# A decoder layer in split fp32: query tiles one by one with one step of Strassen's products behind each, in place of pairs of tiles with up to three steps

## The chip, the cores and the metric

One NeuronCore of a Trainium2 chip. The metric is the device time of one execution in microseconds, the median of three runs: 1028.97 (1028.85 to 1028.97). One more execution was profiled; its trace is what the views below show. TensorE is called PE, its weight loads PEld, VectorE DVE, ScalarE ACT, GpSimd POOL, SyncE (which issues most of the loads) SP.

## What is computed

One decoder layer on x (256 tokens by 2048), fp32. Cut to what matters here:

```python
proj = jnp.einsum('btd,dc->btc', x, w_in[l])
(q_lat, c_kv, attn_gate, q_idx, k_idx, w_idx,
 x_rnn, rnn_gate, g_a, g_b) = jnp.split(proj, SPLIT_POINTS, axis=-1)
...
attn = _sparse_attention(q_lat, c_kv, q_idx, k_idx, w_idx, rel_bias, w_uv[l])
branch_a = jnp.einsum('btc,cd->btd', attn * jax.nn.silu(attn_gate), w_branch_a[l])
h = _rglru(x_rnn, conv_w[l], conv_b[l], w_gate_a[l], b_gate_a[l],
           w_gate_x[l], b_gate_x[l], lru_lambda[l])
branch_b = jnp.einsum('btc,cd->btd', h * jax.nn.silu(rnn_gate), w_branch_b[l])
merged = jax.nn.sigmoid(g_a) * branch_a + jax.nn.sigmoid(g_b) * branch_b
sub = jnp.einsum('btd,de->bte', merged, w_out[l])
x = _layernorm(ALPHA * x + sub, ln_g[l], ln_b[l])
```

`q_lat` has 16 heads of 256 columns, 32 tiles of 128 columns. The merge gates `g_a` and `g_b` have 2048 columns each, four chunks of 512.

## The kernel before

**Split products.** Every fp32 factor is split into a high part (`hi_of`, a copy on ACT, line 116) and a low part (`lo_of`, a subtraction on DVE, line 120), and a product is hi·hi + hi·lo + lo·hi. A weight piece of 128 x 1024 is loaded by SP into one of four buffers "raw" (512 KB), split into one of five buffers "hi" and one of five "lo", and used by PE. `halves` (line 183) is the list of all pieces in the order of use. `load_to(n)` and `split_to(n)` (lines 204 and 254) issue loads and splits up to piece n; the callers keep splits five pieces and loads nine pieces ahead of PE, which is what the buffers allow. Each engine executes its own instructions in the order in which the program emits them.

**The order of work.** `col_jobs` lists the stages: indexer queries (qi), attention gate (ag), queries (q), two chunks of gate A (ga), branch A (ba), RG-LRU input (xr), two chunks of gate B (gb), RG-LRU gate (rg), branch B (bb), then the output projection. Small work (evictions, the heads' softmax, sums) is written as generators on an agenda: `spawn(t, gen)` puts one at a tick, `tick(t)` runs what is due and moves it on at each `yield`. A tick is a quarter of a tile (eight matmuls) in the tile stages and six matmuls in the chunks. D0 is the first tick of the query stage.

**The query stage.** `pair` (line 1145) does two tiles of 128 columns together: eight runs of eight matmuls, first the four with the high weights (512 columns moving: x high and x low), then the four with the low weights (256 columns moving). The high and low buffers of a pair's four pieces come free in the last four runs. A tile's result is evicted by `post_q`, and `head(h)` (line 601) starts at D0 + 8h + 20: logits (`psl`, ten matmuls), softmax on DVE and ACT, transposes (`pspT`) nine ticks on, the product with the values (`pspv`) sixteen ticks on. `values(g)` (line 562) makes the values of four heads: twelve matmuls into two banks (`psv`), then a split on ACT (`vh`) and DVE (`vl`) in the next two ticks. It stands at the start of tile 8g + 6.

**Strassen's products in the query stage.** One chunk of gate A and one of gate B are computed not as chunks but by seven block products, four jobs of steps: j1 and j2 (eight steps of two products), j3 (four steps), j4 (eight). A step is six matmuls (`quarter_step`, line 943). `quarters(pair)` gives the steps behind each pair: 0, 0, 0, 2, 2, 2, 2, 0, 3, 3, 2, 2, 2, 3, 2, 3. The weight sums that they need are made by `sums` on DVE into eight tiles "form" or in the raw buffer; the sums of x by `early_sums`, and by `late_sum` (three operations on POOL with two scratch tiles, then a split) for j3. `quarter_sums` makes those for the next chunk, out of eight form tiles that `load_quarters` loads again over POOL's queue.

**Banks.** PSUM has eight banks: 0 to 3 for results of tiles and chunks (`accs`), 4 to 7 for the rest (`auxs`), each list used in rotation. While j1 to j4 run, bank 3 and bank 7 are taken out of the lists (at the first step) and hold the products; `after_j1` to `after_j4` (lines 968 to 1002) combine them, and after_j4 puts both banks back at the head of their lists.

Of the kernel before, what the change touches and what calls it, by code (L numbers as in the profile page):

```python
# [90 lines left out]
def layer(ctx, tc, ar, out):  # L93
# [90 lines left out]
    for job in jobs:  # L184
        if job[0] == "q" and job[1] % 8 == 6:
            where["uv", job[1] // 8] = len(halves)
            halves.append(("wuv", job[1] // 8, 0))
        for pc in range(8 if job[0] in CHUNKS else 2):
            step = seven(job) and (seven(job)[0], seven(job)[1][pc])
            if step and step[1] is not None:  # L190
                where[step] = len(halves)
                halves += [(step[0] + e, step[1], 0) for e in "ab"]
            where[job, pc] = len(halves)
            halves.append(("w" + job[0], job[1], pc) if job[0] in CHUNKS else ("wt", tiles.index(job), pc))
        if job[0] == "q" and job[1] % 2:
            for step in quarters(job[1] // 2):
                where[step] = len(halves)
                halves.append((*step, 0))
# [5 lines left out]
    def load_to(n):  # L204
        while st["load"] < min(n, len(halves)):
            i = st["load"]
            kind, a, s = halves[i]
            st["load"] += 1
            if kind in ("s1b", "s2b"):
                continue  # L210
            if kind == "s1a":
                nc.sync.dma_start(form[a], ar["wgb"][0, 4 + a // 2, :, a % 2, :])
            raw = wpool.tile([P, 1024], F32, name=f"raw{i}", tag="raw", bufs=4)
            raws[i] = raw
            if kind in ("j2", "j4"):
                src = ar["wgb"][3] if kind == "j2" else ar["wga"][2]
                nc.sync.dma_start(raw[:, :512], src[4 + a // 2, :, a % 2, :])
                continue
            if kind == "wt":
                src = ar["wt"][a, :, s * 8:(s + 1) * 8, :].rearrange("p k c -> p (k c)")  # L220
            elif kind == "j1":
                src = ar["wj"][a].rearrange("p k c -> p (k c)")
            elif kind == "j3":
                src = ar["wga"][2, a].rearrange("p k c -> p (k c)")
# [10 lines left out]
    def sums(i):  # L235


        kind, k, _ = halves[i]
        raw = raws[i]
        if kind == "j1":  # L240
            return nc.vector.tensor_sub(form[k], raw[:, 512:], raw[:, :512])
        if kind == "j2":
            return nc.vector.tensor_sub(form[k], raw[:, :512], form[k])
        if kind == "j3":
            for e in range(2):
                c = slice(e * 512, (e + 1) * 512)
                nc.vector.tensor_sub(raw[:, c], form[2 * k + e], raw[:, c])
            return
        if kind == "j4":
            return nc.vector.tensor_sub(raw[:, 512:], form[k], raw[:, :512])  # L250
        nc.vector.tensor_sub(raw[:, 512:], raw[:, 512:], raw[:, :512])
        nc.vector.tensor_sub(form[k], form[k], raw[:, 512:])

    def split_to(n):
        while st["split"] < min(n, len(halves)):
# [17 lines left out]
            else:  # L273
                if kind == "s1b":
                    raw = raws.pop(i - 1)
                    nc.vector.tensor_sub(raw[:, 512:], form[k], raw[:, :512])
                    src = [(slice(0, 512), form[k]), (slice(512, 1024), raw[:, 512:])]
                elif kind in ("j1", "j2"):
                    src = [(slice(0, 512), raws.pop(i)[:, :512]), (slice(512, 1024), form[k])]
                elif kind == "s2b":  # L280
# [568 lines left out]
    def load_quarters(n):  # L849

        x = []
        for j in range(8):
            x.append(gate_tile(f"form{n}_{j}", "form"))
            form[j] = x[j]
            nc.gpsimd.dma_start(x[j].rearrange("p (k t) -> p k t", k=2),
                                ar["xT"][2 * j:2 * j + 2].rearrange("k p t -> p k t"))
        return x
# [8 lines left out]
    def quarter_sums():  # L866

        x = load_quarters(1)
        yield 12

# [5 lines left out]
        for j in range(4):  # L876
            yield (1, 3, 4, 2)[j]
            dst = [p for tag in homes[j] for p in piece(tag, 2, 1 if tag in ("bias", "pa") else 2)]
# [19 lines left out]
    def early_sums():  # L898

        x = load_quarters(0)  # L900
        yield 16
        homes = {(s, j): slot(f"sj{s}_{j}").rearrange("p (k e t) -> p k e t", k=2, e=2)
                 for s, j in [(1, j) for j in range(4)] + [(s, j) for j in range(4) for s in (2, 4)]}
        for j in range(4):
            yield 3
            a11, a21, a12, a22 = four(x, j)
# [13 lines left out]
    def late_sum(j):  # L920

        d, e = (rows2(tmp_tile(f"s3{i}_{j}", "s")) for i in "de")
# [45 lines left out]
    def after_j1():  # L968
        for n, p in (("a", 1), ("c", 5)):
            cq[n] = gate_tile(f"cq_{n}")  # L970
            nc.scalar.activation(cq[n], psj[p], AF.Copy)
            yield 9

    def after_j2():

        cq["b"] = gate_tile("cq_b")
# [3 lines left out]
        yield 8  # L980
        cq["d"] = gate_tile("cq_d")
        nc.vector.tensor_add(cq["d"], psj[3], cq["c"])

    def after_j3():

        nc.vector.tensor_add(cq["b"], psj[7], cq["b"])
        yield
        nc.vector.tensor_add(cq["c"], psj[7], cq["c"])

    def after_j4():  # L990

        nc.vector.tensor_add(cq["a"], psj[2], cq["a"])
        yield
        nc.vector.tensor_sub(cq["b"], cq["b"], psj[4])
        accs.insert(0, 3)
        auxs.insert(0, 7)
        gates["gb", 3, 0], gates["gb", 3, 1] = cq["d"], cq["c"]
        yield 20
        for t, n in enumerate("ab"):
            gates["ga", 2, t] = cq[n]  # L1000
            nc.scalar.activation(cq[n], cq[n], AF.Sigmoid)
            yield
# [142 lines left out]
    def pair(kind, i):  # L1145

        t0 = at[kind, i]
        if kind == "q" and i % 8 == 6:
            spawn(t0, values(i // 8))
        pss = [acc_tile(f"ps_{kind}{i + e}") for e in range(2)]  # L1150
        for qt in range(8):
# [14 lines left out]
            if not high and half:  # L1166
                spawn(t + 1, posts[kind](i + e, pss[e]))
        if kind == "q":
            for job, k in quarters(i // 2):
                if (job, k) == ("j1", 0):  # L1170
                    accs.remove(3)
                    auxs.remove(7)
                quarter_step(job, k)
                if k == (3 if job == "j3" else 7):
                    spawn(t0 + 8, after[job]())

    for kind, i in jobs:
        if kind in CHUNKS:
            chunk(kind, i)
        elif i % 2 == 0:  # L1180
            pair(kind, i)
# [228 lines left out]
```

## Time and profile before

| | us |
|---|---|
| median of three runs | 1028.97 |
| profiled execution | 1027.56 |
| its span, first to last instruction | 1025.8 |
| PE busy | 1006.9 |
| DVE busy | 780.7 |
| ACT busy | 594.9 |
| POOL busy | 127.9 |
| mean granted clock of PE | 0.994 |

The query stage runs from 159.8 to 420.5 us of the span, gate A's two chunks follow. Rows of the view of waits read: who waited, `<-` for whom, us in total, times, longest. Rows of the timeline: start, duration, engine, line, operation, out<-in, and in brackets the idle time before it and what ended it. Rows of the windows: the stretch, its length, then busy us (and instructions) of PE, PEld, DVE, ACT and POOL, the granted clock, the busy share of the DMA engines and GB/s. Rows of groups: busy us, mean ns of one, and the idle time before. Rows of the chain: start, duration, what. Rows of loads: KB each and the median us from issue to landing.

### The profile page before, as it was taken

To read this page: it belongs to the slowest core of one execution; us is meant where nothing else is said; L and a number is where in the kernel's file an instruction comes from. 1 tells how busy PE (TensorE), PEld (TensorE's weight loads), DVE (VectorE), ACT (ScalarE), POOL (GpSimd) and SP (SyncE) were. 2 spreads that over 40 slices of the span, in tenths; PEclk is the share of its full clock that TensorE was granted. 3 is DMA by queue.
4 is the path that set the end of the run, shared out by engine and by line. 5 is a ranking of instruction groups with operands and counts; after the bars stand their busy time and mean duration, and the time that the engine had idled before them with its cause. 6 is when DMAs were issued, how large, how long until landed. Compare 5 with 4: busy or idle time off the path is not lost.

```text
span 1025.8 us, 14984 instructions
## 1 busy us (share of the span) xinstructions
PE 1006.9 (98%) x5320; PEld 867.4 (85%) x5320; DVE 780.7 (76%) x1306; ACT 594.9 (58%) x1014; POOL 127.9 (12%) x166
## 2 busy tenths in 40 slices
PE   9999999999999899799999999999999999999997
PEld 8898888888898788688888888888888888888885
DVE  5587887878778988658988868888678875655685
ACT  6566645666766566566555555555885554544452
POOL 0015341110102220300000000000252000000002
PEclk9999999999999999899999999999999999999999
DMA  9755886667556556745767676655555668766652
GB/s 307 252 165 177 307 309 204 191 186 241 166 177 195 185 166 203 266 144 191 220 217 217 204 230 188 191 191 192 179 182 166 202 211 327 224 185 184 195 175 82
DMA packets 65067, 210.08 MB, mean 205 GB/s; under 512 B 7120, under 2 KB 14160, under 8 KB 63968
## 3 DMA queue, kind: packets, MB, share of 16 engines
q1 hardware_dynamic: 61664, 195.32, 59.7%
q0 software_dynamic: 2608, 12.88, 3.4%
q8 instruction: 42, 0.69, 0.3%
q10 hardware_dynamic: 720, 0.92, 0.3%
q14 instruction: 33, 0.27, 0.1%
HBM read 206.96 MB, written 6.32 MB: 208 GB/s over the span
## 4 chain that ended last, share of the span: by engine, by line
PE 87%; DVE 5%; ACT 4%; issue 2%; DMA 1%; POOL 0%; DVEq 0%; ACTq 0%; POOLq 0%
PE ps_q L299 15%; PE ps_ag L299 9%; PE ps_xr L299 9%; PE ps_rg L299 5%; PE ps_ba L1096 3%; PE ps_bb L1096 3%; PE ps_bb L1095 3%; PE ps_ba L1097 3%; PE ps_ba L1095 3%; PE ps_bb L1097 3%; PE psq L299 2%; PE ps_qi L299 2%; PE pso L1095 2%; PE pso L1096 2%; PE pso L1097 2%; DVE lo L120 2%
## 5 line engine op out<-in xcount | busy, mean ns | idle before, releaser
L120 DVE TENSOR_TENSOR lo<-raw,hi 128x1024 fp32r<-128x1024 f32 x348 | 418.4, 1209 | 185.8 <-ACT hi L116 170.5
L116 ACT ACTIVATE hi<-raw 128x1024 fp32r<-128x1024 f32 x348 | 350.2, 1029 | 166.7 <-PE pso L1097 25.3
L299 PE MATMUL ps_q<-xs,hi 128*128 128x512 f32 x512 | 118.8, 389 | 0.0
L299 PEld LDWEIGHTS ps_q<-xs,hi 128*128 128x128 f32 x512 | 95.9, 188 | 19.8
L299 PE MATMUL ps_q<-xs,lo 128*128 128x256 f32 x512 | 69.2, 284 | 0.0
L299 PEld LDWEIGHTS ps_q<-xs,lo 128*128 128x128 f32 x512 | 65.2, 191 | 1.2
L299 PE MATMUL ps_rg<-xs,hi 128*128 128x512 f32 x256 | 60.2, 391 | 0.6 <-ACT hi L116 0.6
L299 PE MATMUL ps_ag<-xs,hi 128*128 128x512 f32 x256 | 60.0, 390 | 0.0
L299 PE MATMUL ps_xr<-xs,hi 128*128 128x512 f32 x256 | 59.6, 390 | 0.0
L299 PEld LDWEIGHTS ps_rg<-xs,hi 128*128 128x128 f32 x256 | 47.5, 188 | 11.0 <-ACT hi L116 1.5
L299 PEld LDWEIGHTS ps_xr<-xs,hi 128*128 128x128 f32 x256 | 47.6, 188 | 9.6
L299 PEld LDWEIGHTS ps_ag<-xs,hi 128*128 128x128 f32 x256 | 47.5, 188 | 9.5
L556 POOL TENSOR_TENSOR bias<-bias,mask 128x256 f32<-128x256 f32 (+1 forms) x32 | 27.0, 865 | 191.4 <-DMA bias<-dz 75.1
L1095 PE MATMUL ps_bb<-hi,ub 128*128 128x512 f32 x128 | 50.4, 393 | 0.0
L1097 PE MATMUL ps_ba<-hi,ua 128*128 128x512 f32 x128 | 49.9, 390 | 0.0
L1096 PE MATMUL ps_ba<-lo,ua 128*128 128x512 f32 x128 | 49.9, 390 | 0.0
L1097 PE MATMUL ps_bb<-hi,ub 128*128 128x512 f32 x128 | 49.9, 390 | 0.0
L1096 PE MATMUL ps_bb<-lo,ub 128*128 128x512 f32 x128 | 49.9, 389 | 0.0
L1095 PE MATMUL ps_ba<-hi,ua 128*128 128x512 f32 x128 | 49.8, 389 | 0.0
L1095 PE MATMUL pso<-hi,xs 128*128 128x512 f32 x96 | 37.5, 391 | 0.0
L1097 PE MATMUL pso<-hi,xs 128*128 128x512 f32 x96 | 37.4, 389 | 0.0
L1096 PE MATMUL pso<-lo,xs 128*128 128x512 f32 x96 | 37.4, 389 | 0.0
(424 smaller groups left out, 2062.9 us busy)
## 6 DMA issues: line engine op xcount, KB each, us to landing
raw<-in_wt SPq DMA_DIRECT2D x168, 512.0 KB, 4.8
raw<-in_wba SPq DMA_DIRECT2D x32, 512.0 KB, 3.8
raw<-in_wbb SPq DMA_DIRECT2D x32, 512.0 KB, 4.3
raw<-in_wo SPq DMA_DIRECT2D x32, 512.0 KB, 3.5
raw<-in_wga SPq DMA_DIRECT2D x20, 512.0 KB, 4.0
raw<-in_ws SPq DMA_DIRECT2D x16, 512.0 KB, 4.5
raw<-in_wgb SPq DMA_DIRECT2D x16, 512.0 KB, 4.0
wr<-in_wA SPq DMA_DIRECT2D x14, 424.0 KB, 4.9
```

The lines of the kernel that those rows point to most:

```text
L116: nc.scalar.activation(hi, src, AF.Copy)
L120: nc.vector.tensor_sub(lo, src, f(hi))
L299: nc.tensor.matmul(ps[:, :n], w, rhs[:, :n], start=start, stop=stop)
L556: nc.gpsimd.tensor_add(b[:, r, :W[r]], b[:, r, :W[r]], mask[:, r, :W[r]])
L1095: nc.tensor.matmul(o, mh, hi, start=first and d == 0, stop=False)
L1096: nc.tensor.matmul(o, mh, lo, start=False, stop=False)
L1097: nc.tensor.matmul(o, ml, hi, start=False, stop=d == KT - 1)
```

## The change

- Query tiles are done one by one by `single`: high, low, low, high runs of eight matmuls, so that each piece is done with before the next.
- One step of Strassen's products stands behind each tile from tile 5 on, and one behind tile 3.
- The steps of j2 and j4 share loads: the even step loads 512 KB for itself and the odd one (before: 256 KB each). j4 makes its difference in the form tile and splits two halves of 512 columns.
- The results of j1 are kept in two "slot" tiles, and the gates get tiles of their own when their values exist; after_j4 puts bank 7 at the end of the list, and banks 3 and 7 leave the lists at tile 0.
- `load_quarters` issues its eight loads two at a time, three ticks apart; early_sums starts at D0 - 30 in place of D0 - 16.
- `values` moves to the start of tile 8g + 4, `head` starts two ticks earlier, late_sum uses one scratch tile and other ticks, the constants of the RG-LRU come 30 ticks later, and the POOL multiplications in `roots` are spread.

The diff, cut to its core:

```diff
-def quarters(pair):
+def quarters(i):
-    n = (0, 0, 0, 2, 2, 2, 2, 0, 3, 3, 2, 2, 2, 3, 2, 3)
-    return steps[sum(n[:pair]):sum(n[:pair + 1])]
+    return steps[:1] if i == 3 else steps[i - 4:i - 3] if i > 4 else []
...
-        if job[0] == "q" and job[1] % 8 == 6:
+        if job[0] == "q" and job[1] % 8 == 4:
             where["uv", job[1] // 8] = len(halves)
...
-            if kind in ("s1b", "s2b"):
+            if kind in ("s1b", "s2b") or kind in ("j2", "j4") and a % 2:
                 continue
...
-                nc.sync.dma_start(raw[:, :512], src[4 + a // 2, :, a % 2, :])
+            elif kind in ("j2", "j3", "j4"):
+                src = {"j2": ar["wgb"][3, 4 + a // 2], "j3": ar["wga"][2, a], "j4": ar["wga"][2, 4 + a // 2]}[kind]
...
         if kind == "j4":
-            return nc.vector.tensor_sub(raw[:, 512:], form[k], raw[:, :512])
+            return nc.vector.tensor_sub(form[k], form[k], half)
...
         nc.vector.memset(w[:, :, 0:1], 1.0)
+        yield 6 * q
         for n in range(4 * q, 4 * q + 4):
-            yield
+            yield 2 if q else 1
             nc.gpsimd.tensor_mul(v[:, n, :], v[:, n, :], ri[n][:, T:])
...
+        for m in range(4):
+            for j in (m, m + 4):
+                nc.gpsimd.dma_start(rows2(x[j]), ar["xT"][2 * j:2 * j + 2].rearrange("k p t -> p k t"))
+            yield 3
...
-        nc.gpsimd.tensor_sub(e, x[2], x[3])
-        nc.gpsimd.tensor_add(d, d, e)
+        nc.gpsimd.tensor_add(d, d, x[2])
+        nc.gpsimd.tensor_sub(d, d, x[3])
...
     def after_j1():
         for n, p in (("a", 1), ("c", 5)):
-            cq[n] = gate_tile(f"cq_{n}")
+            cq[n] = slot(f"cq_{n}", F32)
             nc.scalar.activation(cq[n], psj[p], AF.Copy)
-            yield 9
+            yield
...
     def after_j4():
-        nc.vector.tensor_add(cq["a"], psj[2], cq["a"])
-        yield
+        c11 = gates["ga", 2, 0] = gate_tile("ga2_0")
+        nc.vector.tensor_add(c11, psj[2], cq["a"])
         nc.vector.tensor_sub(cq["b"], cq["b"], psj[4])
         accs.insert(0, 3)
-        auxs.insert(0, 7)
+        auxs.append(7)
...
-    spawn(D0 - 16, early_sums())
-    for j, pair in enumerate((11, 11, 12, 12)):
-        spawn(D0 + 8 * pair - (4 if j < 2 else -1) + j % 2, late_sum(j))
-    spawn(at["ga", 0] + 3, quarter_sums())
+    spawn(D0 - 30, early_sums())
+    for j, t in enumerate((76, 79, 83, 87)):
+        spawn(D0 + t, late_sum(j))
+    spawn(at["ga", 0] + 2, quarter_sums())
...
-    spawn(D0 + 20, lru_consts())
+    spawn(D0 + 50, lru_consts())
...
-        spawn(D0 + 8 * h + 20, head(h))
+        spawn(D0 + 8 * h + 18, head(h))
...
+    def single(i):
+        t0 = at["q", i]
+        if i % 8 == 4:
+            spawn(t0, values(i // 8))
+        if i == 0:
+            accs.remove(3)
+            auxs.remove(7)
+        ps = acc_tile(f"ps_q{i}")
+        for qt, high in enumerate((True, False, False, True)):
+            t, half = t0 + qt, qt // 2
+            seams(t)
+            n = where[("q", i), half]
+            w = parts[n][0 if high else 1]
+            for kk in range(8):
+                mm(ps, w[:, kk * P:(kk + 1) * P], xs[:, half * 8 + kk, :], high, qt + kk == 0, qt == 3 and kk == 7)
+            if qt % 2:
+                parts.pop(n)
+            tick(t)
+            split_to(n + (6 if qt % 2 else 5))
+            load_to(n + (10 if qt % 2 else 9))
+        spawn(t0 + 4, post_q(i, ps))
+        for job, k in quarters(i):
+            quarter_step(job, k)
+            if k == (3 if job == "j3" else 7):
+                spawn(t0 + 4, after[job]())
```

More of the change, by code (lines that the diff above doesn't have):

```diff
@@ L194, in layer @@
             halves.append(("w" + job[0], job[1], pc) if job[0] in CHUNKS else ("wt", tiles.index(job), pc))
-        if job[0] == "q" and job[1] % 2:
-            for step in quarters(job[1] // 2):
+        if job[0] == "q":
+            for step in quarters(job[1]):
                 where[step] = len(halves)
@@ L214, in load_to @@
             raws[i] = raw
-            if kind in ("j2", "j4"):
-                src = ar["wgb"][3] if kind == "j2" else ar["wga"][2]
-                nc.sync.dma_start(raw[:, :512], src[4 + a // 2, :, a % 2, :])
-                continue
             if kind == "wt":
@@ L222, in load_to @@
                 src = ar["wj"][a].rearrange("p k c -> p (k c)")
-            elif kind == "j3":
-                src = ar["wga"][2, a].rearrange("p k c -> p (k c)")
+            elif kind in ("j2", "j3", "j4"):
+                src = {"j2": ar["wgb"][3, 4 + a // 2], "j3": ar["wga"][2, a], "j4": ar["wga"][2, 4 + a // 2]}[kind]
+                src = src.rearrange("p k c -> p (k c)")
             elif kind in ("s1a", "s2a"):
@@ L238, in sums @@
         kind, k, _ = halves[i]
+        if kind in ("j2", "j4") and k % 2:
+            i = next(n for n in reversed(range(i)) if halves[n][:2] == (kind, k - 1))
         raw = raws[i]
+        half = raw[:, k % 2 * 512:(k % 2 + 1) * 512]
         if kind == "j1":
@@ L242, in sums @@
         if kind == "j2":
-            return nc.vector.tensor_sub(form[k], raw[:, :512], form[k])
+            return nc.vector.tensor_sub(form[k], half, form[k])
         if kind == "j3":
@@ L277, in split_to @@
                     src = [(slice(0, 512), form[k]), (slice(512, 1024), raw[:, 512:])]
-                elif kind in ("j1", "j2"):
+                elif kind == "j1":
                     src = [(slice(0, 512), raws.pop(i)[:, :512]), (slice(512, 1024), form[k])]
+                elif kind in ("j2", "j4"):
+                    n = i if k % 2 == 0 else next(n for n in reversed(range(i)) if halves[n][:2] == (kind, k - 1))
+                    raw = raws.pop(n) if k % 2 else raws[n]
+                    src = [(slice(0, 512), raw[:, k % 2 * 512:(k % 2 + 1) * 512]), (slice(512, 1024), form[k])]
                 elif kind == "s2b":
@@ L849, in load_quarters @@
     def load_quarters(n):
[L851 to L856, printed above, removed]
+        x = [gate_tile(f"form{n}_{j}", "form") for j in range(8)]
+        form.update(enumerate(x))
+        for m in range(4):
+            for j in (m, m + 4):
+                nc.gpsimd.dma_start(rows2(x[j]), ar["xT"][2 * j:2 * j + 2].rearrange("k p t -> p k t"))
+            yield 3
         return x
@@ L866, in quarter_sums @@
     def quarter_sums():
-        x = load_quarters(1)
-        yield 12
+        x = yield from load_quarters(1)
         def piece(tag, bufs, n=1):
@@ L876, in quarter_sums @@
         for j in range(4):
-            yield (1, 3, 4, 2)[j]
+            yield (2, 3, 4, 2)[j]
             dst = [p for tag in homes[j] for p in piece(tag, 2, 1 if tag in ("bias", "pa") else 2)]
@@ L898, in early_sums @@
     def early_sums():
-        x = load_quarters(0)
-        yield 16
+        x = yield from load_quarters(0)
+        yield 8
         homes = {(s, j): slot(f"sj{s}_{j}").rearrange("p (k e t) -> p k e t", k=2, e=2)
@@ L904, in early_sums @@
         for j in range(4):
-            yield 3
+            yield 2
             a11, a21, a12, a22 = four(x, j)
@@ L920, in late_sum @@
     def late_sum(j):
-        d, e = (rows2(tmp_tile(f"s3{i}_{j}", "s")) for i in "de")
+        d = rows2(tmp_tile(f"s3d_{j}", "s"))
         x = [f(xs[:, 2 * j:2 * j + 2, c:c + P]) for c in (0, P, T, T + P)]
         nc.gpsimd.tensor_sub(d, x[0], x[1])
-        nc.gpsimd.tensor_sub(e, x[2], x[3])
-        nc.gpsimd.tensor_add(d, d, e)
+        nc.gpsimd.tensor_add(d, d, x[2])
+        nc.gpsimd.tensor_sub(d, d, x[3])
         yield 2
@@ L969, in after_j1 @@
         for n, p in (("a", 1), ("c", 5)):
-            cq[n] = gate_tile(f"cq_{n}")
+            cq[n] = slot(f"cq_{n}", F32)
             nc.scalar.activation(cq[n], psj[p], AF.Copy)
-            yield 9
+            yield
     def after_j2():
-        cq["b"] = gate_tile("cq_b")
+        cq["b"] = gates["ga", 2, 1] = gate_tile("ga2_1")
         nc.vector.tensor_add(cq["b"], psj[6], cq["a"])
@@ L979, in after_j2 @@
         nc.gpsimd.tensor_add(cq["c"], cq["c"], cq["b"])
-        yield 8
-        cq["d"] = gate_tile("cq_d")
-        nc.vector.tensor_add(cq["d"], psj[3], cq["c"])
+        yield 2
+        gates["gb", 3, 0] = gate_tile("gb3_0")
+        nc.vector.tensor_add(gates["gb", 3, 0], psj[3], cq["c"])
     def after_j3():
@@ L987, in after_j3 @@
         yield
-        nc.vector.tensor_add(cq["c"], psj[7], cq["c"])
+        gates["gb", 3, 1] = gate_tile("gb3_1")
+        nc.vector.tensor_add(gates["gb", 3, 1], psj[7], cq["c"])
     def after_j4():
-        nc.vector.tensor_add(cq["a"], psj[2], cq["a"])
-        yield
+        c11 = gates["ga", 2, 0] = gate_tile("ga2_0")
+        nc.vector.tensor_add(c11, psj[2], cq["a"])
         nc.vector.tensor_sub(cq["b"], cq["b"], psj[4])
         accs.insert(0, 3)
-        auxs.insert(0, 7)
-        gates["gb", 3, 0], gates["gb", 3, 1] = cq["d"], cq["c"]
+        auxs.append(7)
         yield 20
-        for t, n in enumerate("ab"):
-            gates["ga", 2, t] = cq[n]
-            nc.scalar.activation(cq[n], cq[n], AF.Sigmoid)
+        for g in (c11, cq["b"]):
+            nc.scalar.activation(g, g, AF.Sigmoid)
             yield
@@ L1147, in pair @@
         t0 = at[kind, i]
-        if kind == "q" and i % 8 == 6:
-            spawn(t0, values(i // 8))
         pss = [acc_tile(f"ps_{kind}{i + e}") for e in range(2)]
@@ L1167, in pair @@
                 spawn(t + 1, posts[kind](i + e, pss[e]))
[L1168 to L1175, printed above, removed]
+    def single(i):
[23 more added lines that the diff above has]
+                spawn(t0 + 4, after[job]())
     for kind, i in jobs:
@@ L1179, in layer @@
             chunk(kind, i)
+        elif kind == "q":
+            single(i)
         elif i % 2 == 0:
```

## The prediction

> **What bounds the kernel now.** I read the engine table of the page first:
>
> ```profile
> PE 1006.9 (98%) x5320; PEld 867.4 (85%) x5320; DVE 780.7 (76%) x1306; ACT 594.9 (58%) x1014; POOL 127.9 (12%) x166
> ```
>
> TensorE (PE) is busy 1006.9 of 1025.8 us. The change adds and removes no matmul, so it can only move the 18.9 us in which PE stands, and the clock that PE is granted. The view of waits, for PE alone, says where PE stands:
>
> ```profile
> PE psl L305 <- DVE cq_b L994: 5.2, 1, 5.2
> PE pspv L650 <- DVE vl L120: 2.8, 1, 2.8
> PE psj L961 <- DVE pb L120: 1.3, 1, 1.3
> PE psj L962 <- DVE lo L120: 1.1, 1, 1.1
> ...
> PE ps_rg L299 <- ACT hi L116: 0.6, 1, 0.6
> ```
>
> The first four lie in the query stage or at its end and make 10.4 us. Next the windows, for the load of the query stage and the granted clock (the column behind POOL) around the longest wait:
>
> ```profile
> 140.00:159.80 19.80, 19.80 (x121) 17.68 (x120) 13.31 (x28) 9.79 (x16) 3.62 (x4) 1.00 0.89 314
> 213.90:420.50 206.60, 202.49 (x1165) 178.41 (x1164) 168.68 (x343) 132.88 (x281) 36.20 (x43) 1.00 0.60 189
> 428.00:432.00 4.00, 0.11 (x1) 0.00 (x0) 2.21 (x5) 3.09 (x9) 0.00 (x0) 0.79 0.96 373
> 432.00:434.00 2.00, 0.67 (x3) 0.67 (x4) 1.27 (x4) 1.81 (x5) 0.00 (x0) 0.50 0.91 306
> 434.00:436.00 2.00, 2.00 (x10) 1.96 (x10) 1.89 (x3) 1.16 (x3) 0.26 (x1) 0.50 0.44 116
> 436.00:438.00 2.00, 2.00 (x9) 1.71 (x8) 2.00 (x5) 0.53 (x2) 1.87 (x2) 0.71 0.84 213
> ```
>
> The means of 0.79, 0.50, 0.50 and 0.71 are a half clock for 1.7 + 2 + 2 + 1.2 = 6.8 us, from about 430.3 to 437.2. In the 206.6 us before it, with a wait of 2.8 us in them, the clock stays at 1.00. So the half clock belongs to the 5.2 us wait, and costs on top of it half of the time that PE works at it. These rows of the timeline give that time, and the cause:
>
> ```profile
> 427.72 0.39 PE L1097 MATMUL ps_ga<-hi,xs 128*128 128x512 f32 x1
> 433.33 0.58 PE L305 MATMUL psl<-cT,qs 128*128 128x256 f32 x1 [5.22 <-DVE cq_b L994]
> ```
>
> ```profile
> 425.42 1.06 ACT L116 ACTIVATE hi<-raw 128x1024 fp32r<-128x1024 f32 x1 [4.20 <-DMA raw<-in_wga]
> 428.70 1.06 ACT L116 ACTIVATE hi<-raw 128x1024 fp32r<-128x1024 f32 x1 [2.22 <-DMA raw<-in_wga]
> ```
>
> ```profile
> 416.54 5.82 POOL L855 DMA_DIRECT2D form<-in_xT  x8
> ```
>
> PE works from 433.3 to 437.2 at half clock: 3.9 us, 1.9 us lost. The recoverable total is 10.4 + 1.9 = 12.3 us.
>
> **The change, part by part.** The pace of PE comes from the chain of waits between two waits, where each piece is PE itself:
>
> ```profile
> 229.86 8.21 PE ps_q L299 x40
> ...
> 238.77 0.47 PE psl L608 x4
> 239.25 0.23 PE pspv L650
> 239.47 0.12 PE pspv L651
> ...
> 239.82 0.96 PE ps_q L299 x8
> 240.78 0.11 PE pspT L633
> 240.89 0.22 PE pspT L635 x2
> ```
>
> Eight low matmuls are 0.96 us, so the 32 high ones in the first row are 8.21 - 0.96 = 7.25 us: 1.81 us a run of eight, 0.227 us each. A psl is ten matmuls of 0.12 (1.2 us), a pspv 0.23 + 3 x 0.12 = 0.6, a pspT 0.33.
>
> *Tiles one by one.* 32 high and 32 low matmuls become four runs of high, low, low, high. Low runs of eight already stand between psl and pspT in these rows and cost no more per matmul than 0.12, so I put the changes of width at zero. What changes is when the five hi/lo buffers come free: now four of them within the 3.84 us of low runs, then none for 7.25 us; after, one per 1.81 + 0.96 = 2.8 us. Splits and loads follow at the same even pace, and one step of Strassen's products (six matmuls, 1.4 us) stands behind each tile instead of none to three behind each pair.
>
> DVE has to keep up. In 213.9 to 420.5 it is busy 168.7 us for twelve pairs with 26 steps: 14.1 us a pair against 202.5 / 12 = 16.9 us of PE, 83%. With two steps a pair both fall a little, and the share stays. DVE pays a little more for the fourth job: one split of 1024 columns becomes two of 512 there.
>
> ```profile
> L120 DVE TENSOR_TENSOR lo<-raw,hi 128x1024 fp32r<-128x1024 f32 x348 | 418.4, 1209 | 185.8 <-ACT hi L116 170.5 <-PE ps_q L299 10.4 <-issue 3.3
> L116 ACT ACTIVATE hi<-raw 128x1024 fp32r<-128x1024 f32 x348 | 350.2, 1029 | 166.7 <-PE pso L1097 25.3 <-DMA raw<-in_wt 24.4 <-PE ps_bb L1097 24.3
> ...
> L120 DVE TENSOR_TENSOR lo<-form,hi 128x512 fp32r<-128x512 f32 x32 | 22.2, 693 | 0.1
> ...
> L120 DVE TENSOR_TENSOR vl<-psv,vh 128x512 fp32r<-128x512 f32 x8 | 5.1, 678 | 0.4 <-ACT vh L116 0.4
> ```
>
> That is 8 x (2 x 0.693 - 1.209) = 1.4 us over eight tiles, under DVE's 17% of slack; uncovered it would cost at most those 1.4 us.
>
> *The four waits.* (1) 5.2 + 1.9 us: after_j4 put bank 7 at the head of the auxiliary list, so the next psl took it although DVE's read of it (L994) was queued behind splits that waited for loads; those loads shared the DMA engines with eight form loads that POOL had issued in one go. After, bank 7 goes to the end of the list, and the form loads go two at a time, the later ones behind the last bias addition on POOL's queue. Two loads of 256 KB (128 x 512 x 4 bytes) in three quarters of six 0.227 us matmuls each (3 x 1.37 us) ask 128 GB/s; the gate's own 512 KB per 2.73 us ask 192; together 320, below the 373 GB/s that the window shows. I take all 7.1 us as gone. (2) 1.3 us: the first step took bank 7 from a pspT still being read. It now leaves the list at tile 0, sixteen quarters ahead: gone. (3) 1.1 us: late_sum's last hi/lo came late. Its split is now emitted five to six quarters ahead of its step, in place of three to four for the two late ones, with one scratch tile instead of two in tag "s"; its three POOL operations remain three: gone. (4) 2.8 us: with three auxiliary banks the pspv of head 4g-1 reuses the first psv bank of group g, and waited for vl:
>
> ```profile
> 337.98 0.58 ACT L116 ACTIVATE vh<-psv 128x512 fp32r<-128x512 f32 x1
> ```
>
> ```profile
> 342.13 0.67 DVE L120 TENSOR_TENSOR vl<-psv,vh 128x512 fp32r<-128x512 f32 x1
> ```
>
> ```profile
> 342.86 0.50 PE L650 MATMUL pspv<-pa,vh 128*128 128x512 f32 x1 [2.75 <-DVE vl L120]
> ```
>
> This one doesn't go; it moves. After, values() stands at tile 8g+4 and head starts two quarters earlier, so psv, psl, pspv follow in this order again and pspv of head 4g-2 reuses the bank. vl is emitted after the tile's first low run, and the bank is wanted one low run and one psl later: 0.96 + 1.2 = 2.1 us. Now it is two high runs, a low run and a psl: 5.8 us. What stands ahead of vl on DVE, counted from the last psv matmul: the next split, which needs ACT's 1.03 and then 1.21 us; one 256-column addition, half of the 0.69 row or a little more, 0.4; vl's first half, 0.68; in all 3.3 us. PE arrives after 1.81 + 0.96 + 0.96 + 1.2 = 4.9 us. So a DVE that is 1.6 us behind costs nothing, and each further microsecond costs one, three times (g = 1, 2, 3; at g = 0 there is no such head). At g = 1 two copies of after_j1 stand ahead of vh on ACT or right behind it, at g = 2 an addition of after_j2 stands ahead of vl; both cost about 0.7 of that margin. Bounds: 0, and the lag that the row shows now, below in the rivals. DVE at 83% in an even order is nearer to the first: 0.5 us each, 1.5 us.
>
> *The hand-over of banks 3 and 7 between jobs.* Each job now follows the one before it in the next tile. The last result of j1 or j3 is emitted after quarter 1 of the next tile and its bank is wanted after a low and a high run, psl, pspv, pspT and three matmuls: 0.96 + 1.81 + 1.2 + 0.6 + 0.33 + 0.7 = 5.6 us, 4.9 without the 0.68 of the reading itself; from j2 to j3 5.2. Bounds again zero and today's lag; I take 0.3 us in all.
>
> *Loads.* Eight of 256 KB fewer for each of two jobs, eight of 512 KB more, same bytes. The odd step issues no load, and its even neighbour's raw buffer is held over one tile more, so loads still run four pieces ahead. Cost zero, if the 2.8 us pace of splits covers a later landing (rivals).
>
> *The rest.* Half of early_sums, twelve operations of 256 columns on DVE at about 0.4 us (the estimate above), 5 us, moves into the end of the previous stage, where DVE is idle 19.8 - 13.3 = 6.5 us and PE never waits; without that cover it would cost those 5 us. cq in slots instead of gates: a place in memory. lru_consts later, quarter_sums' pauses: the same operations on the same engines. In roots POOL's multiplications spread out, and the first comes one quarter later, with the scan of DVE behind it; the nearest rows are PE's 0.6 us wait in that stage, which may go, and one low run, 0.96, which may be added. I take zero for all of these.
>
> Sum: 12.3 - 1.5 - 0.3 = 10.5 us. The profiled execution took 1027.56 us (span 1025.8 and 1.8 around it), which would become 1017.1; it stood 1.4 under the median, so the median goes from 1028.97 to **1018.5 us**.
>
> On the clock, the Trainium skill (TensorE: Matmul & The Clock Gate, Part 1) lets the half clock end one window of about 3.4 us after work resumes, which makes 1.7 us lost instead of the 1.9 that the rows give; by that the sum is 10.3.
>
> **The rivals.**
>
> *B, late loads.* The landing times are
>
> ```profile
> raw<-in_wj SPq DMA_DIRECT2D x8, 512.0 KB, 3.6
> raw<-in_wgb SPq DMA_DIRECT2D x8, 256.0 KB, 2.9
> ```
>
> so each of eight doubled loads lands 0.7 us later, and with one raw buffer held nothing may hide it: 5.6 us, 1024.1. For it speaks ACT's 4.20 us wait for a load above; against it the DMA share of 0.60 in the query stage.
>
> *C, the slower side: bank hand-over with DVE behind.* vl was due after the second high run of its pair, at 330.6 + 3.6 = 334.2 (the first starts as the last psv ends), and ran at 342.13: 7.9 us behind. If that lag stays, each of three values waits 7.9 + 0.7 - 2.1 = 6.5 us and, being longer than 5.2, also pays 1.9 us of half clock; the hand-overs add 3.0, 2.7 and 3.0. That is 34 us of new waits: 1028.97 - 12.3 + 34 = 1051 us. The point from which it decides is a lag of about 5.2 us, where 3 x 3.8 and 0.7 of hand-overs eat the 12.3. For it: that lag, and the 2.1 us in place of 5.8. Against: the lag arose where ACT and DVE stood for loads while four pieces came due at once.
>
> *D, the wait at the gates is only renamed.* If the gate's loads still land late, PE waits for its own pieces of the gate instead of bank 7, and 7.1 us come back: 1025.6; with another few of these it is no change.
>
> *E.* If more frequent changes of bank made PE idle in short gaps often enough to lose its clock, say once per pair, sixteen times 1.9 us would bring 1018.5 + 30 = 1049. Against it: in 213.9 to 420.5 PE changes its bank with every psl, pspv and step, at 1.00. The same page of the Trainium skill (A second HAM failure mode: psum-queue depth-cycling) describes such a loss in another kernel; no row here shows it.
>
> **How the numbers follow.** Forecast (1016.2 to 1021) 0.70; B 0.08; D 0.10; C 0.10; E 0.02. The low end is the whole 12.3 us and the 0.6 of ps_rg, 1016, less a little: 1015.5. The high end takes in B and D: 1026. C, E and the tail of D stay out. About 0.2%, 2.1 us, can be told from no change: below 1026.9 lie the forecast, B and 0.06 of D, 0.84; above 1031.0 most of C and E, 0.11; between them 0.05.
>
> **What would show it.** Right: PE's waits have no cq_b and no psj rows over 0.5 us, pspv <- vl is at most 1 us three times, the clock of every window between the start and the tail is 1.00, and PE's busy time is about 1005. Wrong: psl or pspv waiting for vl over 2 us (C), ACT waiting for in_wga or in_wgb loads with ps_q waiting for it (B), ps_ga waiting for lo at the start of the gates (D), a clock under 1.00 without a long wait (E).

## The result and the profile after

| us | before | after |
|---|---|---|
| median, with its range | 1028.91 (1027.25 to 1028.97, 4 runs) | 1020.39 (1017.44 to 1020.91, 4 runs) |
| profiled execution | 1027.56 | 1020.15 |
| its span | 1025.8 | 1018.4 |

The ratio is 0.9915, with a 95% interval of 0.9894 to 0.9937: 8.5 us less in the medians, 7.4 in the spans. The forecast was 10.5 us less. The engine table after:

```profile
PE 1006.4 (99%) x5320; PEld 867.4 (85%) x5320; DVE 785.1 (77%) x1314; ACT 597.6 (59%) x1022; POOL 131.9 (13%) x166
```

PE now stands for 1018.4 - 1006.4 = 12.0 us (before 18.9), and is busy 0.5 us less: together the 7.4. The view of waits of PE says which of the four long waits are gone:

```profile
PE pspv L653 <- DVE vl L119: 4.0, 1, 4.0
PE warm L315 <- DVE eps L166: 1.0, 1, 1.0
PE ps_rg L302 <- ACT hi L115: 0.6, 1, 0.6
```

No cq_b, no psj. (The second row is at the kernel's start, the third in the RG-LRU gate.) One wait is left in the query stage, and it has grown from 2.8 to 4.0 us. The windows: the query stage, the gates after it, then two windows of 3.41 us around that wait.

```profile
213.90:420.50 206.60, 202.62 (x1158) 177.77 (x1157) 173.33 (x359) 134.44 (x290) 36.48 (x39) 0.99 0.61 188
420.50:440.00 19.50, 19.50 (x100) 16.58 (x99) 13.78 (x27) 11.93 (x26) 6.34 (x8) 1.00 0.79 255
323.17:326.58 3.41, 0.41 (x2) 0.36 (x3) 3.41 (x6) 1.64 (x3) 1.25 (x2) 1.00 0.40 120
326.58:329.99 3.41, 3.41 (x11) 2.80 (x10) 3.41 (x5) 0.38 (x1) 3.25 (x5) 0.50 0.67 205
```

At the gates, where PE stood 5.2 us and had a half clock, it is busy 19.50 of 19.50 us at full clock. The new half clock follows the wait for vl and costs 3.41 / 2 = 1.7 us. So the wait costs 4.0 + 1.7 = 5.7 us: nearly half of the 12.3 us that the old waits and their half clock had cost.

Its cause stands in the timelines of DVE ahead of vl, of ACT (which makes vh, the half that vl needs), of SP and of PE:

```profile
313.57 2.23 DVE L246 TENSOR_TENSOR raw<-form,raw 128x512 f32<-128x512 f32 x2
315.73 1.21 DVE L119 TENSOR_TENSOR lo<-raw,hi 128x1024 fp32r<-128x1024 f32 x1
...
317.93 2.35 DVE L119 TENSOR_TENSOR lo<-raw,hi 128x1024 fp32r<-128x1024 f32 x2
322.15 1.29 DVE L246 TENSOR_TENSOR raw<-form,raw 128x512 f32<-128x512 f32 x2 [1.87 <-DMA raw<-in_wga]
323.36 1.22 DVE L119 TENSOR_TENSOR lo<-raw,hi 128x1024 fp32r<-128x1024 f32 x1
324.50 0.68 DVE L980 TENSOR_TENSOR ga<-psj,cq_a 128x512 f32<-128x512 f32 x1
325.10 0.41 DVE L389 TENSOR_TENSOR s_q<-ps_q,r_q 128x256 f32<-128x256 f32 x1
325.43 1.28 DVE L119 TENSOR_TENSOR vl<-psv,vh 128x512 fp32r<-128x512 f32 x2
```

```profile
319.80 1.07 ACT L115 ACTIVATE vh<-psv 128x512 fp32r<-128x512 f32 x2
```

```profile
316.97 0.33 SPq L225 DMA_DIRECT2D raw<-in_wga  x1
```

```profile
317.12 1.98 PE L302 MATMUL ps_q<-xs,hi 128*128 128x512 f32 x8
318.94 2.07 PE L302 MATMUL ps_q<-xs,lo 128*128 128x256 f32 x16
...
326.17 0.50 PE L653 MATMUL pspv<-pa,vh 128*128 128x512 f32 x1 [3.98 <-DVE vl L119]
```

The row of 322.15 is `sums` for j3's second step, in the order well ahead of vl. Its load left SP at 316.97, when a raw buffer came free (the split of 315.73 ends at 316.94), and DVE stood for it 1.87 us; the two sums, a split and two more operations came between its landing and vl. vh was ready at 320.9, so it was DVE that held vl. The last psv matmul ends at 317.12, where the ps_q run starts. By the prediction's count vl was due 3.3 - 0.68 = 2.6 us later, at 319.7; it ran at 325.43, 5.7 us behind (that this is also the cost in the paragraph above is chance). With the margin of 1.6 us this makes 4.1, and 3.98 was measured. The load's lateness is 1.87 of the 5.7 us; the rest is the work of DVE, the sums and two splits more than were counted.

### The profile page after: what moved, and what is told of

Read it like the earlier page. It is cut to its first block, busy times and chain, and to the rows that moved or that the text cites. A ratio compares the mean times of both kernels' runs of the same rounds, so it can differ in the third digit from the quotient of the medians.

```text
span 1018.4 us, 15036 instructions
## 1 busy us (share of the span) xinstructions
PE 1006.4 (99%) x5320; PEld 867.4 (85%) x5320; DVE 785.1 (77%) x1314; ACT 597.6 (59%) x1022; POOL 131.9 (13%) x166
## 4 chain that ended last, share of the span: by engine, by line
PE 93%; ACT 3%; DVE 2%; issue 1%; DMA 0%; DVEq 0%; ACTq 0%
PE ps_q L302 17%; PE ps_ag L302 9%; PE ps_xr L302 9%; PE ps_rg L302 6%; PE ps_bb L1097 3%; PE ps_bb L1098 3%; PE ps_ba L1098 3%; PE ps_ba L1099 3%; PE ps_bb L1099 3%; PE ps_ba L1097 3%; PE psq L302 2%; PE ps_qi L302 2%; PE pso L1097 2%; PE pso L1099 2%; PE pso L1098 2%; PE ps_ga L1099 1%
## 5 line engine op out<-in xcount | busy, mean ns | idle before, releaser
L119 DVE TENSOR_TENSOR lo<-raw,hi 128x1024 fp32r<-128x1024 f32 (+1 forms) x348 | 414.6, 1194 | 180.9 <-ACT hi L115 176.8
L115 ACT ACTIVATE hi<-raw 128x1024 fp32r<-128x1024 f32 (+1 forms) x348 | 348.7, 1017 | 155.6 <-PE ps_bb L1099 27.9
L302 PE MATMUL ps_q<-xs,hi 128*128 128x512 f32 x512 | 128.0, 394 | 0.0
L302 PE MATMUL ps_q<-xs,lo 128*128 128x256 f32 x512 | 66.4, 283 | 0.0
L559 POOL TENSOR_TENSOR bias<-bias,mask 128x256 f32<-128x256 f32 (+1 forms) x32 | 29.9, 954 | 202.4 <-DMA bias<-dz 202.4
```

The source lines that it names most:

```text
L115: nc.scalar.activation(hi, src, AF.Copy)
L119: nc.vector.tensor_sub(lo, src, f(hi))
L302: nc.tensor.matmul(ps[:, :n], w, rhs[:, :n], start=start, stop=stop)
L559: nc.gpsimd.tensor_add(b[:, r, :W[r]], b[:, r, :W[r]], mask[:, r, :W[r]])
```

## The experiments

**The theory after the result.** The pspv of head 4g - 2 waits at g = 2 because it reuses psv's first bank, and vl, which reads that bank, is held up on DVE by j3's sum and its load. Rivals: the doubled loads are late, the uneven pace of steps keeps DVE behind, or late operands hold PE up whichever bank it uses. A second question is which part of the change took the wait at the gates away. All twelve experiments are edits of one of the two kernels; "ratio" is against the kernel before as it ran in the same round (1027.45 to 1027.82 us there, 1028.91 beside the result), with its interval.

### At the gates

**1. Bank 7 at the end of the list, alone, in the kernel before.**

```diff
-        auxs.insert(0, 7)
+        auxs.append(7)
```

> The kernel before with one edit: after_j4 puts bank 7 at the end of the auxiliary list. Theory (the order of the list made the 5.2 us wait, and the half clock behind it): psl <- cq_b is gone, no window at half clock at the gates, 7.1 us less, about 1021.9. Rival (the late loads made it, the bank only gave it its name): PE waits at the gates for its own pieces instead, 3 us or more of ps_ga <- lo, 1025 or above.

Measured: 1022.52 us, ratio 0.9948 (0.9935 to 0.996). PE's waits:

```profile
PE pspT L633 <- ACT lg L630: 1.6, 1, 1.6
PE psj L961 <- DVE pb L120: 1.5, 1, 1.5
PE psj L962 <- DVE lo L120: 1.3, 1, 1.3
```

The wait for cq_b and its half clock are gone, though ACT still stood 3.44 and 3.42 us for gate loads. So it was mostly the choice of the bank that PE waited for, and 5.2 us of 1027.67 came back with one word. But the first row is a new wait at the gates, for a softmax copy that stood on ACT behind a late split.

```profile
433.20 0.33 PE L633 MATMUL pspT<-ident,lg 128*128 128x128 f32 x1 [1.63 <-ACT lg L630]
```

So the late loads still cost 1.6 us, though not at the place that the rival named.

**2. The eight form loads two at a time, alone, in the kernel before.**

```diff
-        for j in range(8):
-            ...
-            nc.gpsimd.dma_start(...)
+        for m in range(4):
+            for j in (m, m + 4):
+                nc.gpsimd.dma_start(...)
+            yield 3
```

> The kernel before with one edit: load_quarters issues its eight loads two at a time, three ticks apart (the x sums keep their ticks). Theory of the list: ACT's waits for in_wga loads at the gates (4.2 and 2.2 us) shrink, but DVE's read of bank 7 still stands behind the splits, so psl <- cq_b stays above 3 us and the time within 2 us of before. Rival (the burst of eight loads is the cause): the loads land in time, psl <- cq_b falls below 1.5 us without half clock, about 1023.

Measured: 1022.66 us, 0.9951 (0.9938 to 0.9963). The wait for cq_b is 2.3 us and is still followed by 3.41 us at half clock:

```profile
PE psl L305 <- DVE cq_b L993: 2.3, 1, 2.3
```

In the trace only the first two loads leave early, at 416.43; the other six leave together at 434.33, behind the last bias additions on POOL. The changed kernel does the same, at 417.96 and 432.64. The truth lay between the two expectations: the wait fell below the 3 us of the one, not to the 1.5 of the other.

**3. The eight form loads at once again, in the changed kernel.** For the sums at the gates (n = 1) the loop no longer pauses, and the pause comes behind all eight loads; they leave in one row at 416.94.

```diff
-            yield 3
+            if n == 0:
+                yield 3
+        if n == 1:
+            yield 12
```

> The changed kernel; quarter_sums' eight loads are issued in one go again, the x sums keep their ticks. Theory (bank order and spread loads each suffice at the gates): ACT waits 3 us or more for an in_wga load again, PE waits there less than 1.7 us, the time within 1.5 us of the changed kernel's 1020.4. Rival (only the spread keeps the gates free of waits): PE waits 3 us or more at the gates, 1023.5 or above.

Measured: 1019.75 us, 0.9925 (0.9914 to 0.9937): the time of the changed kernel, and no wait of PE at the gates. Nor did ACT stand 3 us for a gate load there, which falsifies that part of the expectation.

**4. Both gate edits undone in the changed kernel:** the edit of 3, and

```diff
-        auxs.append(7)
+        auxs.insert(0, 7)
```

> The changed kernel with both edits at the gates undone: the eight form loads go out at once, and bank 7 goes back to the head of its list. In the kernel before, either edit alone took away most of the 5.2 us wait of psl for cq_b. Theory: the wait needs both old orders and has nothing to do with how the query tiles are ordered; it returns with 3 to 5 us and one or two stretches of half clock, and the time is 1024 to 1027. Rival: the wait needed DVE and ACT to be behind, which pairs of tiles made; one tile at a time they are not, psl waits for cq_b under 1.5 us without a half clock, and the time stays at 1019.5 to 1021.

Measured: 1019.90 us, 0.9924 (0.9909 to 0.9939). The rival was right. The subtraction that frees bank 7, on DVE, and the psl that takes it, on PE:

```profile
424.63 0.68 DVE L1001 TENSOR_TENSOR ga<-ga,psj 128x512 f32<-128x512 f32 x1
```

```profile
425.37 0.38 PE L308 MATMUL psl<-cT,qs 128*128 128x256 f32 x1
```

Before, the same two stood at 432.60 and 433.33, the query stage ending at 420.55 in the one kernel and 421.05 in the other. DVE is 8 us earlier. SP's loads for the gate, which DVE's splits there need, are earlier too; in the kernel before the first two leave at 407.23 and 408.97, and the third begins this row.

```profile
416.30 15.07 SPq L229 DMA_DIRECT2D raw<-in_wga  x7
```

In this one the first three are

```profile
401.33 7.61 SPq L225 DMA_DIRECT2D raw<-in_wga  x3
```

and the third leaves at 408.61, 7.7 us sooner.

**5. As 4, with the pause of after_j4 back as well.** (The expectation calls 4 "the run before last but one".)

```diff
         nc.vector.tensor_add(c11, psj[2], cq["a"])
+        yield
         nc.vector.tensor_sub(cq["b"], cq["b"], psj[4])
```

> The kernel of the run before last but one (the change with both edits at the gates undone), and in it also the pause between the two operations of after_j4 put back, which the change took out. Theory: without that pause both operations stand ahead of the next split in DVE's queue, and this is what kept psl from waiting there (its bank was read at 424.63 to 425.31 and wanted at 425.25). With the pause the split of 427.08 to 428.31 comes first: psl <- the subtraction waits 2.5 to 4 us, with one stretch of half clock, and the time is 1023 to 1026. Rival: the order of the tiles alone keeps DVE early enough: the wait is under 1 us, no half clock, 1019 to 1021.

Measured: 1019.46 us, 0.9921 (0.9907 to 0.9935). The rival again:

```profile
PE psl L308 <- DVE ga L1002: 0.2, 1, 0.2
```

So the wait at the gates goes without the list, the form loads and the missing pause. Each of the two edits to the list and the form loads removes most of it alone, but in the changed kernel they add nothing that can be measured. What removes it there is in the rest of the change, by 12 most likely the order of the tiles; pairs of tiles with these edits undone were not run, so this is not shown.

This run is also a test of the wait that stayed, since up to the gates it is the changed kernel. In its trace j3's load left at 316.71 and landed sooner:

```profile
320.48 1.29 DVE L246 TENSOR_TENSOR raw<-form,raw 128x512 f32<-128x512 f32 x2 [0.45 <-DMA raw<-in_wga]
```

```profile
324.49 0.51 PE L653 MATMUL pspv<-pa,vh 128*128 128x512 f32 x1 [2.27 <-DVE vl L119]
```

DVE stood 0.45 us for it in place of 1.87, and PE waited 2.27 us in place of 3.98, with no half clock. So the landing of one load makes nearly half of the wait; the rest is there without it.

### The wait that stayed

**6. j3's sum emitted right before its own split, not one split ahead.**

```diff
-            if i + 1 < len(halves) and halves[i + 1][0] in ("s1a", "j1", "j2", "j3", "j4"):
+            if kind == "j3":
+                load_to(i + 1)
+                sums(i)
+            if i + 1 < len(halves) and halves[i + 1][0] in ("s1a", "j1", "j2", "j4"):
```

> The changed kernel; the weight sums of j3 are emitted right before their own split, not one piece ahead. Theory (vl at g = 2 stands on DVE behind a j3 sum that waits for its load): pspv <- vl falls from 4.0 to about 0.6 us, the half clock behind it (1.7 us) goes, about 1015.3. Rival (DVE is behind there by its own work, or the 2.1 us budget of the bank is too short in general): the wait stays at 3 us or more, 1019 or above.

Measured: 1018.37 us, 0.9907 (0.9892 to 0.9922); pspv waits 2.4 us, again with 3.41 us of half clock. DVE no longer stands for the load, but ACT stands for a sum:

```profile
318.52 2.96 ACT L115 ACTIVATE hi<-raw 128x1024 fp32r<-128x1024 f32 x3 [4.08 <-DVE raw L246]
322.34 1.07 ACT L115 ACTIVATE vh<-psv 128x512 fp32r<-128x512 f32 x2
```

vh stands behind three splits, the first of which needs the sum of j3's first step, made only at 317.07 here. The theory held only in part: the obstacle moved from DVE's queue to ACT's.

**7. `values` at tile 8g + 2,** in place of 8g + 4: both the line that places its pieces and the one that spawns it.

```diff
-        if i % 8 == 4:
+        if i % 8 == 2:
             spawn(t0, values(i // 8))
```

> The changed kernel with values() at tile 8g + 2 in place of 8g + 4: the same order of banks and the same budget of 2.1 us, but no j3 step near. Theory (the j3 load makes the wait): pspv <- vl below 0.5 us at every g, no half clock in the query stage, about 1014.7. Rival (the budget of the bank): waits of 1 to 4 us come back at one g or more, 1017 to 1021.

Measured: 1015.72 us, 0.9881 (0.9868 to 0.9895), no half clock. What PE waits for in the query stage:

```profile
PE psj L964 <- DVE gb L992: 0.7, 1, 0.7
...
PE pspv L653 <- DVE vl L119: 0.4, 1, 0.4
```

**8. The first psv bank of a group from the result banks.** The order of all work stays, only the bank is another.

```diff
-        pss = [aux_tile(f"psv{g}_{s}") for s in range(2)]
+        pss = [acc_tile(f"psv{g}_0"), aux_tile(f"psv{g}_1")]
```

> The changed kernel with the first of the two psv banks of each group taken from the list of result banks (0 to 2) and not from the auxiliary ones (4 to 6); the order of all work is the same. Theory: what PE waits for in 4.0 us is the bank and not the values, whose first reader comes later. The pspv of head 4g - 2 then finds a free bank, and the wait moves to the next bank of the same kind that vl's second half or the result list holds up: pspv <- vl under 0.5 us, one wait of at most 2.3 us elsewhere, 1016 to 1018.5. Rival: the late DVE holds PE up whichever bank it is (the next ps_q result or pspT waits instead), 3.5 us or more with its half clock, and the time stays at 1019.5 to 1021.

Measured: 1016.27 us, 0.9889 (0.9876 to 0.9903), as the theory said: pspv waits for vl no more, and a shorter wait is at the next bank:

```profile
PE pspT L636 <- DVE vl L119: 2.1, 1, 2.1
```

PE has no wait for the late values themselves; it is the bank that holds it up.

**9. Two steps behind every odd tile,** none behind the even ones.

```diff
-    return steps[:1] if i == 3 else steps[i - 4:i - 3] if i > 4 else []
+    return steps[i - 5:i - 3] if i > 4 and i % 2 else []
```

> The changed kernel; two steps behind every second tile (from tile 5) in place of one behind each, tiles still one by one. Theory (an even pace of splits and loads removes the waits): PE's waits in the query stage grow by 2 us or more against the changed kernel's 4.0, 1022 or above. Rival (the pace of steps doesn't matter, the 24 buffers' order does): PE's waits stay at 4 us or fall, 1020.4 or below.

Measured: 1016.61 us, 0.9893 (0.988 to 0.9905). My expectation was that an uneven pace costs time, and that fell (3 and 11, of the same round, took 1019.75 and 1020.00). The wait at g = 2 is 1.9 us here, with a half clock: DVE stands only 0.15 us for j3's load, but its sums still come ahead of vl. That one step follows each tile is not what gains.

**10. 7 and 9 together,** in `col_jobs`' places and `single` for the one, in `quarters` for the other.

```diff
-        if i % 8 == 4:
+        if i % 8 == 2:
...
+    return steps[i - 5:i - 3] if i > 4 and i % 2 else []
```

> The changed kernel with values() at the start of tile 8g + 2 (before this 8g + 4) and two steps of the products behind every odd tile from 5 on. Each alone took 3.8 to 4.7 us off. Theory: both remove the same wait of pspv for vl, so together they give little more than the earlier values alone: no half clock, PE's waits in the query stage under 1 us in sum, 1014.5 to 1016. Rival: two steps at a time put four splits in a row on DVE and ACT and bring a wait of their own where j3 ends, 1 to 3 us, and the time is 1016.5 to 1019.

Measured: 1014.75 us (1014.28 to 1015.4), 0.9875 (0.9861 to 0.9888), the fastest kernel of this study. The query stage:

```profile
213.90:420.50 206.60, 206.36 (x1181) 180.89 (x1181) 175.00 (x364) 139.65 (x294) 31.53 (x39) 1.00 0.63 195
```

PE stands 0.24 us in 206.6. Its two edits do not add up: against the changed kernel they take off 3.5 and 2.3 us alone and 4.1 together by the ratios (4.7, 3.8 and 5.6 by the medians). Both act on the same wait.

### Loads and tiles

**11. Own loads of 256 KB for j2 and j4,** as in the kernel before, with its `sums` and `split_to` for these jobs.

```diff
-            if kind in ("s1b", "s2b") or kind in ("j2", "j4") and a % 2:
+            if kind in ("s1b", "s2b"):
...
+                nc.sync.dma_start(raw[:, :512], src[4 + a // 2, :, a % 2, :])
```

> The changed kernel; every step of j2 and j4 loads its own 256 KB again into a raw buffer of its own. Theory (sharing the loads costs and gains nothing): within 1.5 us of 1020.4, pspv <- vl still 2 us or more. Rival B (a raw buffer held over a tile makes loads late, the j3 load among them): pspv <- vl below 1.5 us and no half clock there, about 1015 to 1017.

Measured: 1020.00 us, 0.9924 (0.9911 to 0.9937). pspv still waits 3.7 us. Sharing the loads neither gains nor costs.

**12. Tiles in pairs, everything else as changed.** The pair's function takes over what `single` does for values, banks and steps; two steps stand behind each pair.

```diff
-        elif kind == "q":
-            single(i)
...
+        for job, k in quarters(i + 1) if kind == "q" else []:
+            quarter_step(job, k)
```

> The changed kernel with its query tiles in pairs again (four runs of high, four of low), two steps behind each pair from pair 2 on, all the rest as changed. Theory (one tile at a time is what keeps DVE, ACT and the loads even): PE waits 4 us or more beyond the changed kernel's, 1023 or above. Rival (banks, slots, spread loads and earlier starts make the gain, the tiles don't): within 1.5 us of 1020.4 or below it.

Measured: 1026.80 us (1024.06 to 1031.33, 12 runs), 0.9989 (0.9974 to 1.0003): no difference from before. The profiled execution took 1031.33, the longest of them; its waits:

```profile
PE pspv L653 <- DVE vl L119: 9.7, 3, 4.6
PE psj L964 <- ACT hi L115: 1.3, 1, 1.3
...
PE psj L965 <- DVE lo L119: 1.0, 2, 0.8
```

With pairs vl is late three times. And at the gates ACT stands for loads again (7.0 us between 400 and 440, in the view of waits; 0.2 us from 213.9 to 440 in the changed kernel):

```profile
ACT hi L115 <- DMA raw<-in_wga: 7.0, 4, 3.1
```

The rest of the change, taken together, is worth nothing that can be measured without tiles one by one. This does not say that each part is worth nothing: with the new place of `values` the waits for vl are 9.7 us here, 2.8 in the kernel before.

## Why the prediction was right, and where it was off

- *The four waits: right in their sum.* 5.2 + 1.9, 1.3 and 1.1 us are gone, and the fourth stands in the new place that was named. Of (1) the credit was wrongly given: bank 7 at the end of the list and the spread form loads would each remove most of it (1 and 2), but 4 and 5 show that it goes without them. So the 7.1 us came out right for a reason that was not needed, which is partly luck. The wait (2) for pb stays in 1 and 2 and is gone in 12, which fits bank 7 leaving its list earlier. Of (3) the row was read too simply. Its `lo` is the low part of the step's weights; late_sum's tile is `spare`, and it stood ahead of their split on ACT, where it waited for POOL's last operation. In the kernel before:

```profile
362.67 0.42 ACT L116 ACTIVATE spare<-s3d 128x256 fp32r<-128x256 f32 x1 [1.93 <-POOL s3d L926]
```

```profile
364.50 1.54 DVE L120 TENSOR_TENSOR lo<-raw,hi 128x1024 fp32r<-128x1024 f32 x1 [0.96 <-ACT hi L116]
```

  So (3) was already what the fourth wait became, an operation that waits ahead of a needed one in an engine's queue. Which edit removed it was not tried alone.
- *The term that was mis-sized: "0.5 us each, 1.5 us" for vl at g = 1, 2, 3.* It measured 0, 5.7 and 0, with the half clock. The budget of 2.1 us and the margin of 1.6 were right; at g = 1 and 3 vl ran 0.67 and 0.22 us behind the count (from psv's end at 250.51 and 389.66), within the margin:

```profile
253.78 1.29 DVE L119 TENSOR_TENSOR vl<-psv,vh 128x512 fp32r<-128x512 f32 x2 [0.37 <-ACT vh L115]
```

  What failed is the list of what stands ahead of vl on DVE: a split, an addition and vl itself, with 0.7 us for an addition of after_j2. At g = 2 there were three splits, and two sums for j3 that waited for a load. That is rival C's mechanism, at one place of three, and by the prediction's own sign (a wait for vl over 2 us) it is C that showed there; its half clock of 1.9 us was 1.7. The prediction set the bounds "0, and the lag that the row shows now" and chose near 0; the lag, 5.7 us here too, was nearer to the other end, 7.9.
- *The sum.* 12.3 less 5.7 is 6.6 us; measured in the spans are 7.4, where 10.5 were forecast. The 0.8 us over it: PE's busy time without the half clock falls 0.3 us (1006.9 - 1.9 to 1006.4 - 1.7), and its standing without the long waits 0.5 (18.9 - 10.4 to 12.0 - 4.0), in gaps too short for rows of their own. They were not forecast, and they make the miss smaller.
- *Hand-over of banks 3 and 7: 0.3 forecast, none seen.* Experiment 7, with PE earlier, shows one of 0.7 us.
- *No cost of width changes: right.* In the chain after, a high, a low and a low run stand as one piece:

```profile
250.67 3.72 PE ps_q L302 x24
```

  That is 1.81 + 2 x 0.96 = 3.73 us, by the rows of before.
- *DVE's extra 1.4 us for the fourth job:* the row of 1209 ns mixes two shapes. The 324 splits of 1024 columns took 1244 ns each, which makes the extra 1.1 us.
- *B, late loads:* refuted by 11 for the sharing; but one load, j3's, late for its buffer and not for its size, made nearly half of the 4 us wait.
- *D and E:* the gates' windows show no renamed wait (experiment 1 shows one of 1.6 us), and the 0.99 of the query stage is the one window of 3.41 us (half of it is 0.8% of 206.6). *C* is what eats the gain in 12, with pairs.
- *The roots' wait* of 0.6 us stayed as it was.
- *The half clock.* The Trainium skill (TensorE: Matmul & The Clock Gate, Part 1) made its cost 1.7 where the rows made 1.9. The rows below count it: before, PE works 0.43 + 3.42 us at half clock, 1.9 lost; after, 3.41, 1.7 lost. Both happen, by where in a window the work resumes.

## What to carry to other kernels

When PE is at 98%, list its waits and ask for each which bank or buffer it wants, and what stands ahead of the operation that frees it in that engine's queue, transfers included: two sums and their late load ahead of a bank's last reader were worth 4 us of waiting here. When an order is changed, count anew the budget between two uses of a bank (2.1 us in place of 5.8 here), and put the producer early enough or give it another bank (7 and 8). Undo the edits of a change one by one and together: here several of them each removed the same wait.

## What the runs showed of the hardware

A wait of 2.75 us left the clock alone in the kernel before, and one of 1.90 us in experiment 9 cost 3.41 us of half clock. The stretches of half clock are 3.41 us or twice that, and lie on a grid of 3.41 us that runs on through the kernel (in every trace they begin a whole number of 3.413 us after the first change of the clock). Windows on that grid, by PE's busy time, the first number after the length. Before, the wait of 2.75 us lies over two windows, and that of 5.22 us fills most of two:

```profile
338.19:341.60 3.41, 1.92 (x17) 1.72 (x15) 3.41 (x6) 1.65 (x4) 1.44 (x1) 1.00 0.64 225
341.60:345.02 3.42, 2.16 (x17) 2.12 (x18) 2.14 (x5) 1.85 (x4) 0.97 (x2) 1.00 0.52 117
426.94:430.35 3.41, 1.17 (x6) 0.63 (x4) 1.36 (x2) 1.65 (x4) 0.00 (x0) 1.00 1.02 388
430.35:433.76 3.41, 0.43 (x2) 0.43 (x3) 2.92 (x7) 3.01 (x9) 0.00 (x0) 0.50 0.88 322
433.76:437.18 3.42, 3.42 (x16) 3.23 (x16) 3.07 (x4) 1.79 (x4) 1.44 (x1) 0.50 0.59 121
```

Experiment 9, whose wait lies in one window:

```profile
321.18:324.60 3.42, 1.52 (x9) 1.20 (x8) 3.42 (x6) 2.16 (x5) 2.09 (x3) 1.00 0.82 245
324.60:328.01 3.41, 3.41 (x11) 2.64 (x11) 2.69 (x4) 0.89 (x1) 2.69 (x3) 0.50 0.82 219
```

Experiment 5, where vl's wait of 2.27 us lies over two again:

```profile
319.72:323.13 3.41, 2.50 (x22) 2.30 (x20) 2.96 (x5) 2.04 (x4) 0.00 (x0) 1.00 0.91 286
323.13:326.55 3.42, 2.06 (x11) 1.78 (x12) 3.42 (x5) 0.97 (x3) 2.83 (x3) 1.00 0.77 233
326.55:329.96 3.41, 3.41 (x18) 2.82 (x17) 3.41 (x5) 2.06 (x3) 3.33 (x4) 1.00 0.56 177
```

Experiment 12, the first of the windows that its longest wait for vl (4.6 us, at g = 2) touches:

```profile
323.80:327.21 3.41, 1.78 (x13) 1.50 (x11) 3.23 (x6) 2.56 (x6) 0.00 (x0) 1.00 0.44 134
```

In all fourteen traces, up to the last stage, a window with PE busy 1.52 us or less (45%) was followed by one at half clock, and none with 1.78 us or more (52%) was; between them nothing was seen. In the last stage, where PE runs out of work, two windows of 1.89 and 1.98 us were followed by half clock, so the busy time is not quite what is counted. The Trainium skill (TensorE: Matmul & The Clock Gate, HAM oscillation) gives its rule as no gaps of PE over about 3.4 us; the traces do not agree, a gap of 1.90 us is enough if it lies in one window. The free-running window of the Trainium skill (same page, Part 1) agrees with them, and makes the loss a matter of where the grid falls in a run. This may be why the changed kernel's runs lie at 1017.44 and at 1020.15 to 1020.91: the mean granted clock was 0.999 in the first and 0.997 to 0.998 in the others, where one window at half clock takes 0.0017. How soon j3's load lands (experiment 5) is the other part of it. Neither was tried by itself.

The two sums at 313.57 took 2.23 us for two and those at 322.15 took 1.29; POOL ran late_sum's operations beside the former and nothing beside the latter. In the same trace the 41 splits of 128 x 1024 that ran beside an operation of POOL took up to 1.75 us, and the 275 others at most 1.35. The slow sums stand ahead of the split that frees the buffer for j3's load, so up to 0.9 us of that load's lateness may come from them. That POOL slows DVE was not tried by itself.
